# One layer of a streaming encoder in float32: S4 of the Strassen weights by an addition on VectorE, and another order of the down products

## The chip, the cores and the metric

The kernel runs on 1 core of one Trainium2 chip. The metric is the device time of one execution in microseconds (us); the figure that counts is the median over runs. TensorE (PE) multiplies, VectorE (DVE) and ScalarE (ACT) work on elements, GpSimd (POOL) and SyncE (SP) mostly issue transfers here.

## The reference, cut to what matters

One layer on 512 tokens of width 1024: a half-step SwiGLU feed-forward, a mixer (state-space scan and chunked attention), a second half-step feed-forward, a final norm. The change touches the two feed-forwards alone:

```python
def swiglu(h, w_gate, w_up, w_down):
    return (jax.nn.silu(h @ w_gate) * (h @ w_up)) @ w_down

x = x + 0.5 * swiglu(rms_norm(x, ffn1_norm[i]), ffn1_w_gate[i], ffn1_w_up[i], ffn1_w_down[i])
x = x + hybrid_mixer(x, ...)
x = x + 0.5 * swiglu(rms_norm(x, ffn2_norm[i]), ffn2_w_gate[i], ffn2_w_up[i], ffn2_w_down[i])
```

All of it is float32, with 2816 hidden columns.

## The kernel before, in words

**Products.** Every float32 product is made of three TensorE products of a high and a low part (high x high, high x low, low x high). The high part of a weight unit is a cast by ACT (line 272), the low part a subtraction on VectorE (line 274). Both write a ring of four pairs of tiles named xw (`usplit`, lines 267 to 275), so the cast for a unit has to wait until the unit four before it has been multiplied.

**Seven products for eight.** The 2816 hidden columns are cut into 11 blocks d of two tiles. A block's gate and up weights form a 2 x 2 matrix of units A11, A12, A21, A22 of 512 KB each. The first two blocks of the first feed-forward and the first of the second are multiplied plainly (A11 to A22); all others by the Winograd form of Strassen's scheme, with seven products P1 to P7 whose weights are A11 (P1), A12 (P2), A22 (P4), S1 = A21 + A22 (P5), S2 (P6: S1 and A11), A11 and A21 (P7) and S4 (P3: S2 and A12). The signs lie in how the arrays are laid out and in the operands. The down weights go the same way, as units of two blocks, in three groups of blocks: 0 to 3, 4 to 7 and 8 to 10. The first feed-forward does two of these groups so, the second all three.

**Where the sums are made.** `ffn_weights` (line 309) makes a Job for each product: a list of transfers, and a split. A plain unit is loaded by SP into one of four buffers named raw (`whole`, line 323). S1 is loaded by SP into a quarter of the view buffers (tiles s40 and s52; `first`, line 329) and added to by a transfer that POOL issues with an accumulate (`more`, line 332). S2 adds A11 to the same view by another such transfer, after S1 has been split; S4 adds A12 to it by a third, after S2 has been split. P7's weights are made by adding to P1's raw buffer. A12 is thus read twice from memory: once into a raw buffer for P2, and once for S4.

**The order.** `program` (line 281) writes the products out by hand. In the gate/up blocks they are P5, P1 of block d, P3, P4 of block d - 1, P6, P2, P7 of block d. In the down groups 0 and 1 they follow DOWN (line 279), every product as a pair of units, with P3 and P4 of the last gate/up block and P5 and P1 of the next one put between. Each turn calls `Stream.get`, which splits the units up to three products ahead (`look`; two ahead within a pair) and starts transfers whose lead (the numbers 5, 6, 7, 12 in `product`) has come, if the job that has to be split first has been. This is the order of the text; the order on each engine, and the points at which the queues of SP and POOL take a transfer, are set from it by the framework's own plan when the kernel is built.

**What multiplies.** `run` (line 545) does one gate/up product: 24 matmuls of 256 columns (line 555) into one of three PSUM banks of the block: P1, P6, P7 and P4 into X, P2 into L, P5 and P3 into H. After P1 and after P6 ACT copies the bank out (lines 560 and 563), and the next product of that bank waits for it. `down` (line 604) does the down products, 12 matmuls of 512 columns for a unit (lines 142 to 144), and VectorE adds finished banks to x (line 628).

Of the kernel before, what the change touches and what calls it, by code (L numbers as in the profile page):

```python
# [12 lines left out]
ALU = mybir.AluOpType  # L13
# [24 lines left out]
def hybrid_block(ctx: ExitStack, tc, xT, xt, par, wgu1, wd1, ws1, win, wdt, wv, wo, rbt, wgu2, ws2, fin, out):  # L38
    nc = tc.nc
    V, S, G, T = nc.vector, nc.scalar, nc.gpsimd, nc.tensor  # L40
# [4 lines left out]
    def sb(tag, shape, dt=F32, bufs=1):  # L45
        uid[0] += 1
        return pool.tile(shape, dt, tag=tag, name=f"{tag}_{uid[0]}", bufs=bufs)
# [9 lines left out]
    def f(ap):  # L57
        return ap.bitcast(F32)
# [51 lines left out]
    class Stream:  # L110
# [16 lines left out]
        def get(self):  # L127
            i = self.used
            self.used += 1
            while self.done < min(len(self.jobs), i + 1 + self.look):  # L130
                job = self.jobs[self.done]
                job.move(0, True)
                job.parts = job.split()
                self.done += 1
            for n in range(self.done, min(len(self.jobs), i + 18)):
                self.jobs[n].move(n - i)
            return self.jobs[i].parts
# [95 lines left out]
    def wide_tile(g, dt=F32R):  # L233
        if g not in wide or wide[g][0] != dt:
            wide[g] = dt, sb(f"s{g}", [P, GROUPS[g], SEQ], dt)
        return wide[g][1]
# [30 lines left out]
    def usplit(src):  # L267

        i = turn[0] % 4
        turn[0] += 1  # L270
        hi = sb(f"xw{2 * i}", list(src.shape), F32R)
        S.copy(out=hi, in_=src)  # L272
        lo = sb(f"xw{2 * i + 1}", list(src.shape), F32R)
        V.tensor_tensor(out=lo, in0=src, in1=f(hi), op=ALU.subtract)  # L274
        return hi, lo

    DOWN = ("P5", "P1", "P2", "P6", "P7", "P3", "P4")

    def program(plain, by_tokens):


        if plain == 1:
            out = [("A11", 0), ("A21", 0), ("A12", 0), ("P1", 1), ("P5", 1), ("A22", 0), ("P6", 1), ("P2", 1), ("P7", 1)]
        else:
            out = [(a, d) for d in range(plain) for a in ("A11", "A21", "A12", "A22")]
            out += [(p, plain) for p in ("P5", "P1", "P6", "P2", "P7")]
        out = [("P", p, d) for p, d in out]
        ends = [b for _, b in BLOCKS[:2]]  # L290
        for d in range(plain + 1, ND):
            if d - 1 not in ends:
                out += [("P", p, e) for p, e in (("P5", d), ("P1", d), ("P3", d - 1), ("P4", d - 1))]
            out += [("P", p, d) for p in ("P6", "P2", "P7")]
            if d in ends:

                down = [("S", ends.index(d), p, (0, 1)) for p in DOWN]
                out += down[:1] + [("P", p, d) for p in ("P3", "P4")] + down[1:6]
                out += [("P", p, d + 1) for p in ("P5", "P1")] + down[6:]
        last = [("P", p, ND - 1) for p in ("P3", "P4")]  # L300
        if by_tokens == 3:
            return out + [("S", 2, "P5", (0,))] + last + [("S", 2, p, (0,)) for p in ("P1", "P2")] + [
                ("S", 2, p, (1,)) for p in ("P1", "P5")] + [("S", 2, "P6", (0, 1)), ("S", 2, "P2", (1,))] + [
                ("S", 2, p, (0, 1)) for p in ("P7", "P3", "P4")]
        out += [("D", 2, 0, 0)] + last + [("D", 2, 1, 0), ("D", 2, 0, 1), ("D", 2, 1, 1)]
        return out + [("D", 2, o, c) for o in range(2, KD) for c in range(2)]

    def ffn_weights(wgu, plain, by_tokens, wst, wd=None):


        bufs, jobs, views = {}, {}, []
        LAST = (2, ND - 1)

        def view(d):
            if d not in bufs:
                i = views.index(d)
                m = 2 if type(d) is int else min(2, BLOCKS[d[0]][1] - d[1])
                bufs[d] = wide_tile((40, 52)[i // 2 % 2], F32)[:, 2 * (i % 2):2 * (i % 2) + m]
                if type(d) is int:
                    bufs[d] = bufs[d].rearrange("p a (k c) -> p a k c", c=P)  # L320
            return bufs[d]

        def whole(key, src):
            def go():
                bufs[key] = sb("raw", list(src.shape), bufs=4)
                nc.sync.dma_start(out=bufs[key], in_=src)
            return go

        def first(d, src):
            return lambda: nc.sync.dma_start(out=view(d), in_=src)  # L330

        def more(get, src):
            return lambda: G.dma_start(out=get(), in_=src, accum_op=ALU.add)  # L333

        def product(p, d, A):

            sum_ = lambda: view(d)
            raw = {"P1": "g", "P2": "g2", "P4": "u2"}.get(p)
            if p[0] == "A":
                n = ("A11", "A12", "A21", "A22").index(p)  # L340
                j = Job(lambda: usplit(bufs[p, d]), (6, "raw", whole((p, d), A[n])))
            elif raw:
                j = Job(lambda: usplit(bufs[raw, d]), (6 if p == "P1" else 5, "raw",
                                                       whole((raw, d), A[("P1", "P2", "", "P4").index(p)])))
            elif p == "P5":
                views.append(d)
                before = jobs["P3", views[-5]] if len(views) > 4 else jobs.get(("A21", 0))
                j = Job(lambda: usplit(view(d)), (12, before, first(d, A[2])), (7, None, more(sum_, A[3])))
            elif p == "P6" and d == LAST:

                v = d + (2,)
                views.append(v)
                j = Job(lambda: usplit(view(v)), (14, jobs["P3", views[-5]], first(v, A[2])),
                        (10, None, more(lambda: view(v), A[3])), (6, None, more(lambda: view(v), A[0])))
            elif p == "P6":
                j = Job(lambda: usplit(view(d)), (6, jobs["P5", d], more(sum_, A[0])))
            elif p == "P7":
                j = Job(lambda: usplit(bufs["g", d]), (6, jobs["P1", d], more(lambda: bufs["g", d], A[2])))
            else:
                v = d + (2,) if d == LAST else d  # L360
                j = Job(lambda: usplit(view(v)), (6, jobs["P6", d], more(lambda: view(v), A[1])))
            jobs[p, d] = j
            if p == "P7":
                jobs["P1", d].holds = j
            ws.jobs.append(j)

        for step in program(plain, by_tokens):
            if step[0] == "P":
                p, d = step[1:]
                product(p, d, wgu[d])  # L370
            elif step[0] == "S":
                n, p, pieces = step[1:]
                for a in [BLOCKS[n][0] + 2 * c for c in pieces]:
                    product(p, (n, a), [wst[i, :, a:min(a + 2, BLOCKS[n][1]), :] for i in range(4)])
            else:
                n, o, c = step[1:]
                if c == 0:
                    a, b = 2 * BLOCKS[n][0], 2 * BLOCKS[n][1]
                    ws.add(wd[o, :, a:b, :], b - a, P)
                    late = ws.jobs.pop() if (n, o) in ((2, 0), (2, 1)) else None  # L380
                    if late:
                        jobs["late", o] = late
                elif ("late", o) in jobs and n == 2:
                    ws.jobs.append(jobs["late", o])

    class XCombos:
# [40 lines left out]
        def split(self, d, src):  # L427
            S.copy(out=d[0], in_=src)
            V.tensor_tensor(out=d[1], in0=src, in1=f(d[0]), op=ALU.subtract)
# [25 lines left out]
    def ffn(xc, n_plain, early, by_tokens, rc, between, after):  # L455
# [179 lines left out]
        for step in program(n_plain, by_tokens):  # L635
            if step[0] == "S":
# [5 lines left out]
                down(*step[1:])  # L642
                past = step[1:3] == (1, DOWN[-1])
                continue
# [786 lines left out]
```

## Time and profile before

| what | value |
|---|---|
| median of 3 runs | 1032.14 us (1031.85, 1032.14, 1036.27) |
| the profiled execution, its own time | 1035.34 us |
| its span | 1033.6 us |
| TensorE matmul / weight load busy | 1007.9 us (98%) / 888.6 us (86%) |
| VectorE / ACT / POOL busy | 810.2 us (78%) / 587.8 us (57%) / 163.7 us (16%) |
| moved by transfers | 162.66 MB, 60.04 MB of it on the queue that POOL feeds |

The profile is of one execution. Times count from the start of its span. PE rows are matmuls, PEld rows are the weight loads that go beside them. An arrow in brackets names what an engine had waited for. The first feed-forward runs from about 10 to 310 us, the mixer from there to about 660, the second feed-forward to the end.

### The profile page before, as it was taken

How to read it: one execution, taken by the hardware profiler on the slowest of the kernel's cores; microseconds unless marked ns; L12 is line 12 of the kernel's file. 1: busy time of each engine (PE TensorE's matmuls, PEld its weight loads, DVE VectorE, ACT ScalarE, POOL GpSimd, SP SyncE). 2: the span in 40 equal slices, each digit the busy share in tenths (PEclk: the TensorE clock that was granted, in tenths of full speed). 3: DMA queues.
4: the chain of work that ended last, by engine and by line, in shares of the span. 5: the costliest groups of instructions: out<-in, count | busy, mean ns of one | idle time of the engine just before them, and what ended most of it. 6: DMA issues, size and time to landing. Idle time of an engine off the chain costs nothing. (4 is left out here: it accounts for less than half of the span.)

```text
span 1033.6 us, 16129 instructions
## 1 busy us (share of the span) xinstructions
PE 1007.9 (98%) x6154; PEld 888.6 (86%) x6154; DVE 810.2 (78%) x1353; ACT 587.8 (57%) x926; POOL 163.7 (16%) x186
## 2 busy tenths in 40 slices
PE   8999999999999999999999999999999999999895
PEld 7889989998898777778878778879999899988884
DVE  7868876887676698978867999797688668876587
ACT  7555535654474456646656876666655356544445
POOL 1111121111110013323201111101211111111110
PEclk9999999999999999999999999999999999999988
DMA  8969989998652321222232223755898889988842
GB/s 309 290 160 210 218 185 228 224 203 211 147 122 91 102 82 62 71 73 69 71 98 71 82 83 102 230 131 128 191 211 209 196 209 231 209 213 202 167 107 99
DMA packets 48221, 162.66 MB, mean 157 GB/s; under 512 B 5264, under 2 KB 6032, under 8 KB 48144
## 3 DMA queue, kind: packets, MB, share of 16 engines
q0 software_dynamic: 16848, 60.04, 33.2%
q1 hardware_dynamic: 28992, 96.74, 27.1%
q10 hardware_dynamic: 2304, 4.86, 1.5%
q8 instruction: 48, 0.79, 0.3%
q14 instruction: 29, 0.24, 0.1%
HBM read 159.52 MB, written 2.10 MB: 156 GB/s over the span
## 5 line engine op out<-in xcount | busy, mean ns | idle before, releaser
L555 PE MATMUL mm<-s,xw 128*128 128x256 f32 x1824 | 231.6, 284 | 6.4 <-ACT fu L563 4.6
L555 PEld LDWEIGHTS mm<-s,xw 128*128 128x128 f32 x1824 | 224.9, 192 | 7.6 <-ACT fu L563 5.0
L272 ACT CAST xw<-raw 128x1024 fp32r<-128x1024 f32 (+1 forms) x127 | 131.5, 1036 | 138.3 <-PE mm L555 56.0
L274 DVE TENSOR_TENSOR xw<-raw,xw 128x1024 fp32r<-128x1024 f32 (+1 forms) x127 | 152.7, 1204 | 69.4 <-ACT xw L272 69.4
L555 PE MATMUL aux<-s,xw 128*128 128x256 f32 x1368 | 174.5, 283 | 0.6 <-DVE xw L274 0.6
L555 PEld LDWEIGHTS aux<-s,xw 128*128 128x128 f32 x1368 | 169.0, 192 | 1.9 <-DVE xw L274 0.8
L142 PE MATMUL mm<-xw,whi 128*128 128x512 f32 x364 | 149.1, 410 | 0.0
L143 PE MATMUL mm<-xw,whi 128*128 128x512 f32 x364 | 144.3, 397 | 0.0
L274 DVE TENSOR_TENSOR xw<-s,xw 128x1024 fp32r<-128x1024 f32 (+1 forms) x87 | 104.6, 1202 | 50.5 <-ACT xw L272 50.4
L144 PE MATMUL mm<-xw,wlo 128*128 128x512 f32 x364 | 144.0, 396 | 0.0
L272 ACT CAST xw<-s 128x1024 fp32r<-128x1024 f32 (+1 forms) x87 | 90.0, 1035 | 92.1 <-DMA s<-wgu 27.7
L333 POOL DMA_DIRECT2D s<-wgu x57 | 52.1, 934 | 314.6 <-DMA s<-wgu 133.6
L84 ACT CAST whi<-raw 128x512 fp32r<-128x512 f32 (+1 forms) x104 | 62.1, 601 | 65.3 <-PE mm L143 47.2
L86 DVE TENSOR_TENSOR wlo<-raw,whi 128x512 fp32r<-128x512 f32 (+1 forms) x104 | 74.3, 716 | 13.8 <-ACT whi L84 13.2
L142 PEld LDWEIGHTS mm<-xw,whi 128*128 128x128 f32 x364 | 68.5, 188 | 16.2 <-issue 2.2
L144 PEld LDWEIGHTS mm<-xw,wlo 128*128 128x128 f32 x364 | 68.4, 188 | 16.1
L143 PEld LDWEIGHTS mm<-xw,whi 128*128 128x128 f32 x364 | 68.5, 188 | 15.8 <-issue 1.2
L333 POOL DMA_DIRECT2D s<-ws x31 | 27.1, 873 | 163.3 <-DVE xw L274 65.8
L144 PE MATMUL aux<-xw,s 128*128 128x512 f32 x106 | 41.8, 394 | 0.0
L143 PE MATMUL aux<-xw,s 128*128 128x512 f32 x106 | 41.7, 394 | 0.0
L142 PE MATMUL aux<-xw,s 128*128 128x512 f32 x106 | 41.7, 394 | 0.0
L903 POOL TENSOR_TENSOR fu<-dt,tri 128x512 fp32r<-128x512 f32 x16 | 18.9, 1190 | 95.6 <-PE aux L954 45.5
(294 smaller groups left out, 1743.9 us busy)
## 6 DMA issues: line engine op xcount, KB each, us to landing
raw<-wgu SPq DMA_DIRECT2D x68, 512.0 KB, 5.8
s<-wgu POOLq DMA_DIRECT2D x57, 512.0 KB, 6.5
raw<-win SPq DMA_DIRECT2D x28, 512.0 KB, 3.5
s<-ws POOLq DMA_DIRECT2D x27, 512.0 KB, 5.7
raw<-ws SPq DMA_DIRECT2D x27, 512.0 KB, 4.7
s<-wgu SPq DMA_DIRECT2D x19, 512.0 KB, 5.0
raw<-wgu POOLq DMA_DIRECT2D x19, 512.0 KB, 6.2
raw<-wo SPq DMA_DIRECT2D x12, 512.0 KB, 3.7
```

Of the source, the lines that this page charges most:

```text
L84: S.copy(out=hi, in_=src)
L86: V.tensor_tensor(out=lo, in0=src, in1=f(hi), op=ALU.subtract)
L142: T.matmul(ps, lhsT=sh, rhs=mh, start=start, stop=False, skip_group_check=skip)
L143: T.matmul(ps, lhsT=sh, rhs=ml, start=False, stop=False, skip_group_check=skip)
L144: T.matmul(ps, lhsT=sl, rhs=mh, start=False, stop=stop, skip_group_check=skip)
L272: S.copy(out=hi, in_=src)
L274: V.tensor_tensor(out=lo, in0=src, in1=f(hi), op=ALU.subtract)
L333: return lambda: G.dma_start(out=get(), in_=src, accum_op=ALU.add)
L555: T.matmul(ps[:, j * HS:(j + 1) * HS], lhsT=sw[:, j, k], rhs=m, start=(p in ("P1", "P2", "P5") and j == 0 and k == 0 and n == 0), stop=(k ...
L903: G.tensor_tensor(out=r, in0=f(src[:, c, h0:h0 + 4]).unsqueeze(2).broadcast_to([P, 4, P]), in1=tri.unsqueeze(1).broadcast_to([P, 4, P]), o ...
```

## The change

S4's transfer goes for all gate/up blocks done in seven products and for the down groups 0 and 1 (`here`); the down group 2 keeps it. In its place the split of P2 begins with one VectorE addition of the raw buffer, which holds A12, to the view, which holds S2. For this S2 must have been split already, so in DOWN the product P6 goes ahead of P2; in the gate/up blocks it is there already.

```diff
-    DOWN = ("P5", "P1", "P2", "P6", "P7", "P3", "P4")
+    DOWN = ("P5", "P1", "P6", "P2", "P7", "P3", "P4")
...
             sum_ = lambda: view(d)
+            here = type(d) is int or d[0] < 2
             raw = {"P1": "g", "P2": "g2", "P4": "u2"}.get(p)
...
+            elif p == "P2" and here:
+                def split():
+
+                    V.tensor_tensor(out=view(d), in0=view(d), in1=bufs[raw, d], op=ALU.add)
+                    return usplit(bufs[raw, d])
+                j = Job(split, (5, "raw", whole((raw, d), A[1])))
             elif raw:
...
+            elif here:
+                j = Job(lambda: usplit(view(d)))
             else:
                 v = d + (2,) if d == LAST else d
                 j = Job(lambda: usplit(view(v)), (6, jobs["P6", d], more(lambda: view(v), A[1])))
```

## Rows read from the trace of the kernel before

**Rows 1.** The page's busy time of each engine

```profile
PE 1007.9 (98%) x6154; PEld 888.6 (86%) x6154; DVE 810.2 (78%) x1353; ACT 587.8 (57%) x926; POOL 163.7 (16%) x186
```

**Rows 2.** Stretches of 20 us: length, then busy us of each engine, PEclk, DMA share, GB/s

```profile
680.00:700.00 20.00, 19.45 (x100) 16.67 (x101) 19.96 (x38) 10.31 (x17) 1.74 (x2) 1.00 0.44 102
...
860.00:880.00 20.00, 20.00 (x169) 20.00 (x168) 16.38 (x24) 12.14 (x18) 3.52 (x4) 1.00 0.93 214
...
980.00:1000.00 20.00, 17.39 (x100) 16.07 (x101) 14.06 (x23) 10.23 (x16) 1.73 (x2) 0.83 0.51 118
```

**Rows 3.** Waits of TensorE: us in total, times, longest us

```profile
PE mm L555 <- ACT fu L563: 4.6, 1, 4.6
PE mm L555 <- ACT fa L560: 1.8, 1, 1.8
...
PE aux L205 <- DVE s L198: 0.6, 1, 0.6
```

**Rows 4.** Timeline of TensorE near 978: start us, us, line, operation, [idle before]

```profile
957.71 3.04 PE L555 MATMUL mm<-s,xw 128*128 128x256 f32 x24
...
974.93 3.04 PE L555 MATMUL aux<-s,xw 128*128 128x256 f32 x24
982.61 5.24 PE L555 MATMUL mm<-s,xw 128*128 128x256 f32 x24 [4.64 <-ACT fu L563]
```

**Rows 5.** Timeline of ACT in the same stretch

```profile
981.03 1.04 ACT L272 CAST xw<-s 128x1024 fp32r<-128x1024 f32 x1 [6.35 <-DMA s<-wgu]
981.98 0.58 ACT L563 COPY fu<-mm 128x512 f32<-128x512 f32 x1
```

**Rows 6.** Timeline of POOL in the same stretch

```profile
971.52 0.88 POOL L333 DMA_DIRECT2D s<-ws  x1 [3.73 <-DMA s<-ws]
972.14 1.14 POOL L333 DMA_DIRECT2D s<-wgu  x1
```

**Rows 7.** Stretches of 4 us, columns as in the stretches of 20

```profile
60.00:64.00 4.00, 2.21 (x16) 2.01 (x17) 3.97 (x8) 3.00 (x4) 0.00 (x0) 1.00 0.61 174
...
972.00:976.00 4.00, 4.00 (x35) 4.00 (x35) 4.00 (x9) 2.49 (x5) 1.90 (x3) 1.00 0.79 160
...
980.00:984.00 4.00, 1.39 (x6) 1.39 (x7) 1.89 (x3) 2.97 (x4) 0.00 (x0) 0.57 0.37 73
```

**Rows 8.** The page's transfers: a queue, and issues with us to landing

```profile
q0 software_dynamic: 16848, 60.04, 33.2%
...
s<-wgu POOLq DMA_DIRECT2D x57, 512.0 KB, 6.5
```

**Rows 9.** Timeline of VectorE near 978

```profile
959.24 1.22 DVE L274 TENSOR_TENSOR xw<-s,xw 128x1024 fp32r<-128x1024 f32 x1
```

**Rows 10.** Timeline of VectorE, opening of the first feed-forward

```profile
58.70 1.22 DVE L274 TENSOR_TENSOR xw<-raw,xw 128x1024 fp32r<-128x1024 f32 x1
59.84 0.42 DVE L494 TENSOR_TENSOR fa<-fh,fh 128x256 f32<-128x256 f32 x1
```

**Rows 11.** Waits of VectorE

```profile
DVE xw L274 <- ACT xw L272: 119.8, 89, 5.8
```

**Rows 12.** Timeline of ACT, opening of the first feed-forward

```profile
53.75 1.05 ACT L272 CAST xw<-s 128x1024 fp32r<-128x1024 f32 x1 [7.15 <-DMA s<-wgu]
...
60.29 0.62 ACT L477 CAST s<-fa 128x512 fp32r<-128x512 f32 x1 [1.06 <-DVE fa L494]
...
62.71 0.58 ACT L560 COPY fa<-mm 128x512 f32<-128x512 f32 x1
```

**Rows 13.** Timeline of TensorE, opening of the first feed-forward

```profile
59.97 1.58 PE L555 MATMUL aux<-s,xw 128*128 128x256 f32 x11 [0.63 <-DVE xw L274]
63.34 3.13 PE L555 MATMUL mm<-s,xw 128*128 128x256 f32 x24 [1.79 <-ACT fa L560]
```

**Rows 14.** Timeline of VectorE, opening of the second feed-forward

```profile
699.93 0.15 DVE L169 TENSOR_TENSOR rq_q<-rq_o 128x4 f32<-128x4 f32 x1
...
700.81 0.68 DVE L198 TENSOR_TENSOR s<-ident,rq_h 128x512 fp32r<-128x512 f32 x1
```

## The prediction

> **What bounds the kernel now.** I read the busy shares first: TensorE has work in 98% of the span, VectorE in 78% [rows 1]. A share of 98% can still hide slow feeding, so I read the stretches of 20 us next. From 860 to 880 TensorE and its weight load are both busy for 20.00 of 20 us, beside a DMA share of 0.93; from 680 to 700 and from 980 to 1000 TensorE lacks time, and in the last the granted clock is 0.83 [rows 2]. So a steady gate/up stretch has nothing to give, however many transfers are taken out of it, and what this change can win lies in a few holes. The waits of TensorE name them: one of 4.6 us on ACT's copy of line 563, one of 1.8 us on ACT's copy of line 560, one of 0.6 us on the VectorE work of line 198 [rows 3]. The timeline then says what each hole is made of.
>
> The largest is at the end of the second feed-forward. Products follow each other every 2.87 us (six from 957.71 to 974.93); P2 of column block 10 runs from 974.93, and P7 of 10 should follow near 977.9 but starts at 982.61, and its 24 matmuls then take 5.24 us instead of 3.04 [rows 4]. ACT explains it: the copy that frees P6's bank for P7 starts at 981.98, behind a cast that waited 6.35 us for a transfer into a view buffer [rows 5]. By the order of the splits in the code (P2's turn splits the third product ahead) this cast is that of P3 of 10, and the transfer is the very accumulation that makes S4. POOL issued it at 972.14, queued behind an accumulation for the down weights that waited for its own first transfer until 971.52 [rows 6]. The cast could start 8.9 us later.
>
> **What it costs.** The wait is 4.64 us. The slow matmuls cost another 5.24 - 3.04 = 2.20 us, at a granted clock of 0.57 from 980 to 984 (between the levels of 1.2 and 2.4 GHz) [rows 4, 7]. Together 6.84 us.
>
> **The change part by part.**
>
> *Removed:* the S4 accumulations, one for each gate/up block done in seven products (9 + 10) and one for each of eight units of down blocks 0 and 1: 27 of 512 KB. Of 57 accumulations from the gate/up weights 19 go [rows 8]. They are 14.2 of the 60.0 MB on the software queue, whose packets take 33.2% of the engines' time [rows 8]: about 8 points of DMA share. In the steady stretches that buys nothing, by rows 2. In the hole at 978 it takes away the transfer that ACT waits for: **-6.84 us**. What is late next there? P3's cast then needs only P2's addition. VectorE is busy for 4.00 of 4 us from 972 to 976 [rows 7], so at worst the addition comes behind that burst and leaves a hole of about 1.2 us; at best none. I take none, since the addition stands in the text ahead of P2's own split.
>
> *Added:* 27 additions of 128x1024 on VectorE. The nearest row is the split's subtraction of the same shape: 1.22 us alone, 1.14 us from start to start when another follows [rows 9, 10]. That is 27 x 1.14 to 1.22 = 31 to 33 us of VectorE time, to be hidden. The cover in steady stretches: VectorE idles 119.8 us in 89 places before the subtraction because ACT's cast is still running, 1.35 us each [rows 11], and the addition needs no cast, so it fits there. Where it does not fit there is lead: a subtraction that starts at 959.24 and ends at 960.46 belongs to the product three ahead of the one that starts at 957.71 [rows 4, 9], so of the one at 957.71 + 3 x 2.87 = 966.32, and 5.9 us are spare. Two additions in a row, as in the down blocks, take 2.4 of these. Cost there: nothing.
>
> *Where the cover is gone.* Two places have no idle VectorE.
> - The opening of the first feed-forward. VectorE is busy for 3.97 of 4 us from 60 to 64 [rows 7]. P6 of block 2 waits for ACT's copy at 62.71, which stands on ACT behind a cast (60.29) that waited for VectorE's instruction of line 494 [rows 12, 10]; TensorE waits 1.79 us [rows 13]. P2's addition stands in the text ahead of line 494's, so I move the whole queue by one addition: +1.14 us. Bounds: -1.8 us (the engines' order falls out better and the hole closes) to +3.3 us (1.14 us and the 2.20 us of a fallen clock).
> - The opening of the second. The chain of short operations for the norm runs bare on VectorE from 699.93 on [rows 14], and TensorE waits 0.6 us for its end [rows 3]. The addition can be put between two of them: 0 to +1.14 us, I take half, +0.6.
>
> *New waits.* The addition waits for A12's load; behind it on VectorE stand P2's subtraction and the reads of PSUM by which banks come free. That load waited on its cast before, so it is no later than it was. The cast of P3 now waits for VectorE instead of a transfer, two or more products after the addition.
>
> *Moved.* In the down blocks the P2 pair goes behind the P6 pair: P6's two accumulations on POOL are due two products earlier, P2's two loads on SP as much later, and the banks of P2 are taken and given back later. No wait of TensorE lies in these stretches before [rows 3], and a like sum takes 6.5 us to land [rows 8], against a lead of six products. POOL's queue is passed by nothing that is due sooner. Cost: nothing; bounds 0 to +1.
>
> **The sum** on the profiled execution: -6.84 + 1.14 + 0.6 = -5.1 us, so 1035.34 becomes 1030.2. That execution was 3.2 us above the median of 1032.14, and the runs shown (1031.85, 1032.14, 1036.27) lie at two heights about 4 us apart. If the 3.2 us are part of the hole at 978, a median run has only 3.6 us of it to lose and ends at 1030.2; if they lie elsewhere, it ends at 1027.0. I cannot tell which, and take the middle: **1028.6 us**, with 1026 to 1031 as this case's own range. A measurement of this kernel tells 0.5% (5.2 us) from no change, so the bounds are 1027.0 and 1037.3, and the forecast itself straddles the first.
>
> **A rule against the change.** The trace shows that a hole can be paid for twice: after 4.64 us of waiting the next 24 matmuls ran at a granted clock of 0.57, but from 60 to 64, with waits of 0.63 and 1.79 us, it stayed at 1.00 [rows 7, 13]. The Trainium skill (TensorE: Matmul & The Clock Gate, "What's actually happening") says that the half rate is TensorE's default, from which only activity releases it. By that page a hole that an addition widens may bring the fall along, and the opening of the first feed-forward would then cost an estimated 1.14 + 2.20 = 3.3 us; by the rows so far, 1.14 us. The trace agrees with the page at 978 and shows no fall at 60.
>
> **The rivals.**
> - *The additions meet a saturated VectorE, and the clock falls with the holes they widen* (slower). Place: the two openings. Price: 1.14 + 2.20 us at each, 6.7 us. It decides if the hole at 978 is hardly there in a median run, so that nothing pays for it: 1032.14 + 6.7 = 1038.8. For it: VectorE's 19.96 of 20 us at 680 to 700 [rows 2]. Against: both openings' holes are short so far, and the profile does show the hole at 978. Chance 0.10.
> - *The hole is only handed on.* The next instruction on ACT or VectorE holds the copy up, or another accumulation comes late behind POOL's queue, as this one did [rows 6]. Then -6.84 is given back: 1032.14 to 1034. For it: the order on each engine is not the text's, as P2's 11 matmuls at 59.97 ahead of P6's at 63.34 show [rows 13], so a new order comes with the change. Chance 0.25.
> - *Every hole in the feed-forwards closes*, the 1.79 and 0.63 us too, because less traffic lets P6's sum land sooner: 1032.14 - 6.84 - 2.4 = 1022.9. Against: the late sum there (ACT waits 7.15 us for it at 53.75 [rows 12]) is due before any removed transfer. Chance 0.07.
> - *The change doesn't take the transfers away.* The code leaves no move for P3 where the new case holds, so this has no chance worth naming.
>
> **The numbers.** Forecast 0.58, handed on 0.25, slower 0.10, all closed 0.07. Of the forecast's 0.58 some 0.24 lies below 1027.0. Faster: 0.24 + 0.07 = 0.31. Slower: 0.10. Same: 0.59. The range reaches from 1024 (the forecast with the full hole and no new cost at the openings is 1025.3, and a part of the case in which all closes) to 1035 (the hole handed on, with a bound of 1 us for the moved pair); outside lie most of the slower case and half of the fastest, under 2 in 10.
>
> **What would show it.** Right: 38 accumulations from the gate/up weights instead of 57; no TensorE wait of over 1.2 us near 978 and a granted clock of 1.00 there; VectorE busy for 841 to 843 us; the wait on line 560's copy near 2.9 us; steady stretches still at 20.00 of 20. Wrong: a new TensorE wait of several us behind ACT or VectorE in the down blocks or at an opening, with a granted clock under 1 behind it; or the same hole at 978 with another releaser.

## The result, and the profile after

The median fell from 1033.7 us (9 runs, 1031.85 to 1036.27) to **1028.3 us** (9 runs, 1026.99 to 1029.49): a measured ratio of 0.994, with a 95% interval from 0.9928 to 0.9952 (the two medians alone divide to 0.9948, inside it). The profiled execution took 1027.64 us (span 1025.9) against 1035.34 us (1033.6) before, so 7.7 us of span are to be found. In the kernel after, line 555 has become 564, 560 is 569, 563 is 572, and the addition is line 346.

The page of the kernel after: busy time, a queue, the addition's group, and the accumulations from the gate/up weights.

```profile
PE 1006.1 (98%) x6154; PEld 887.0 (86%) x6154; DVE 841.3 (82%) x1380; ACT 588.3 (57%) x926; POOL 140.2 (14%) x159
...
q0 software_dynamic: 12960, 45.88, 25.9%
...
L346 DVE TENSOR_TENSOR s<-s,raw 128x1024 f32<-128x1024 f32 x27 | 33.0, 1222 | 0.6
...
s<-wgu POOLq DMA_DIRECT2D x38, 512.0 KB, 5.6
```

VectorE has 31.1 us more than in [rows 1], 27 instructions, 33.0 us by the group. The software queue is 14.2 MB lighter than in [rows 8], and 38 accumulations stand where 57 stood. Now the waits of the kernel after (us in total, times, longest), TensorE's and VectorE's:

```profile
PE mm L564 <- ACT fa L569: 1.2, 1, 1.2
...
PE aux L205 <- DVE s L198: 0.6, 1, 0.6
...
DVE xw L274 <- ACT xw L272: 83.9, 81, 6.1
```

The longest wait of [rows 3], 4.6 us on the copy of line 563, has no successor: nothing waits on line 572. VectorE's idle places ahead of the subtraction hold 83.9 us instead of the 119.8 of [rows 11]: 35.9 us less, about the 33.0 that the additions take.

The end of the second feed-forward in the timeline of the kernel after (start, us, engine, line, operation, idle before and what ended it), by engine:

```profile
968.61 5.87 PE L564 MATMUL mm<-s,xw 128*128 128x256 f32 x48
974.31 3.04 PE L564 MATMUL aux<-s,xw 128*128 128x256 f32 x24
977.19 3.04 PE L564 MATMUL mm<-s,xw 128*128 128x256 f32 x24
980.07 0.40 PE L142 MATMUL aux<-xw,s 128*128 128x512 f32 x1
...
974.45 1.05 ACT L272 CAST xw<-s 128x1024 fp32r<-128x1024 f32 x1 [0.39 <-PE mm L564]
975.40 0.58 ACT L572 COPY fu<-mm 128x512 f32<-128x512 f32 x1
...
965.31 1.23 DVE L346 TENSOR_TENSOR s<-s,raw 128x1024 f32<-128x1024 f32 x1
```

P2 of block 10 runs at 974.31 and P7 follows after 2.88 us, without a wait and in 3.04 us. ACT's cast of P3 waits 0.39 us, for a ring buffer, where it waited 6.35 us for a transfer [rows 5]; the copy behind it is done before P2 is. The addition ran at 965.31, nine microseconds ahead of that cast, before VectorE's burst. The stretches of the kernel after (length, busy us of PE, PEld, DVE, ACT, POOL with counts, granted clock, DMA share, GB/s):

```profile
980.00:984.00 4.00, 4.00 (x23) 3.35 (x23) 2.67 (x4) 2.96 (x4) 0.89 (x1) 1.00 0.24 66
980.00:1000.00 20.00, 20.00 (x111) 17.23 (x111) 17.24 (x28) 10.51 (x16) 3.48 (x4) 1.00 0.62 134
860.00:880.00 20.00, 20.00 (x170) 20.00 (x169) 17.37 (x25) 11.93 (x17) 2.60 (x3) 1.00 0.79 184
```

The clock is 1.00 from 980 on, where [rows 7] had 0.57. The steady stretch is at 20.00 as before, with 1 us more of VectorE and a DMA share of 0.79 instead of 0.93 [rows 2]: lighter, and no shorter.

The opening of the first feed-forward, in the same timeline, and one line of the opening of the second:

```profile
52.91 1.05 ACT L272 CAST xw<-s 128x1024 fp32r<-128x1024 f32 x1 [5.72 <-DMA s<-wgu]
...
62.07 0.58 ACT L569 COPY fa<-mm 128x512 f32<-128x512 f32 x1
...
56.34 1.22 DVE L346 TENSOR_TENSOR s<-s,raw 128x1024 f32<-128x1024 f32 x1
...
59.55 1.97 PE L564 MATMUL aux<-s,xw 128*128 128x256 f32 x13
62.70 3.13 PE L564 MATMUL mm<-s,xw 128*128 128x256 f32 x24 [1.19 <-ACT fa L569]
...
699.44 1.23 DVE L346 TENSOR_TENSOR s<-s,raw 128x1024 f32<-128x1024 f32 x1
```

P6 of block 2 starts at 62.70 instead of 63.34 [rows 13]. POOL's issue of the accumulation that P6's sum waits for, in the kernel after and then in the kernel before, and the matmul behind P7 of block 10 in the kernel before:

```profile
44.96 0.87 POOL L333 DMA_DIRECT2D s<-wgu  x1 [1.00 <-DVE fa L509]
```

```profile
44.37 0.88 POOL L333 DMA_DIRECT2D s<-wgu  x1 [0.57 <-DVE fa L500]
...
987.69 0.39 PE L142 MATMUL aux<-xw,s 128*128 128x512 f32 x1
```

**Where the 7.7 us are**, by starts of the same matmuls in both traces: the kernel after is 0.6 us behind when it comes to this opening (53.80 for 53.20), 0.64 ahead at P6, 0.62 ahead still in the last blocks (957.09 for 957.71), 5.42 ahead at P7 of block 10 (977.19 for 982.61) and 7.62 ahead right behind it (980.07 for 987.69). So TensorE wins 1.24 us over the opening, nothing at the second opening, and 4.80 + 2.20 = 7.0 us at the hole. The 0.6 us behind is there from the first products on: TensorE waits 0.99 us for ACT's line 149 at 8.84 us, before 0.39 us. It costs nothing in the end, since P6 waits for its sum anyway; against the kernel before the opening is worth 0.64 us.

### The profile page after: what moved, and what is told of

It is laid out like the page before. It is cut to its first block, busy times and chain, and to the rows that moved or that the text cites. A ratio compares the mean times of both kernels' runs of the same rounds, so it can differ in the third digit from the quotient of the medians.

```text
span 1025.9 us, 16097 instructions
## 1 busy us (share of the span) xinstructions
PE 1006.1 (98%) x6154; PEld 887.0 (86%) x6154; DVE 841.3 (82%) x1380; ACT 588.3 (57%) x926; POOL 140.2 (14%) x159
## 4 chain that ended last, share of the span: by engine, by line
PE 82%; DVE 10%; DMA 3%; ACT 2%; issue 1%; POOL 0%; SPq 0%; ACTq 0%; POOLq 0%; DVEq 0%
PE mm L564 21%; PE aux L564 16%; PE mm L142 10%; PE mm L143 10%; PE mm L144 10%; PE aux L144 3%; PE aux L143 3%; PE aux L142 3%; DMA s<-wgu 2%; DVE fs L857 2%; DVE wlo L86 1%; DMA raw<-wgu 1%; DVE xw L274 1%; PE aux L981 1%; PE aux L772 1%
## 5 line engine op out<-in xcount | busy, mean ns | idle before, releaser
L333 POOL DMA_DIRECT2D s<-wgu x38 | 33.6, 898 | 361.7 <-DMA s<-wgu 115.3
L333 POOL DMA_DIRECT2D s<-ws x23 | 20.0, 869 | 137.1 <-DMA s<-ws 71.4
L346 DVE TENSOR_TENSOR s<-s,raw 128x1024 f32<-128x1024 f32 x27 | 33.0, 1222 | 0.6
```

The source lines that it names most:

```text
L346: V.tensor_tensor(out=view(d), in0=view(d), in1=bufs[raw, d], op=ALU.add)
```

## The experiments

My theory after reading both traces: the whole gain is one transfer of 27, S4 of block 10 in the second feed-forward, and that one only because of its place on POOL's queue. The rivals: less traffic as such; the new order of the down products; and VectorE's additions as a cost hidden in the net.

**The addition for one product alone.** The kernel before, with the new case for block 10 of the second feed-forward only, and DOWN as it was:

```diff
-    DOWN = ("P5", "P1", "P6", "P2", "P7", "P3", "P4")
+    DOWN = ("P5", "P1", "P2", "P6", "P7", "P3", "P4")
...
-            here = type(d) is int or d[0] < 2
+            here = plain == 1 and d == ND - 1
```

> The kernel before, with S4 by addition in one place alone: gate/up block 10 of the second feed-forward (DOWN as before, the other 26 transfers kept). Theory (the gain is the one hole at the end of the second feed-forward, made by this one transfer): 4 to 6 us below the kernel before, a ratio of 0.994 to 0.996; no TensorE wait on the copy of P6's bank near 978, clock 1.00 there. Rival (the gain is 14.2 MB less traffic, spread over 27 transfers): 5.4 / 27 = 0.2 us, a ratio of 1.000.

**All but that one.** The kernel after, with the transfer kept there alone:

```diff
-            here = type(d) is int or d[0] < 2
+            here = (type(d) is int or d[0] < 2) and not (plain == 1 and d == ND - 1)
```

> The changed kernel, with the transfer kept in that one place (block 10 of the second feed-forward) and the other 26 taken away. Theory: the hole near 978 comes back with 2 to 5 us of waiting, and the time is within 1.5 us of the kernel before (ratio 0.998 to 1.001). Rival (traffic): 26/27 of the gain, a ratio of 0.994.

Measured: one addition gives 1027.9 us (1026.82 to 1029.92; before 1035.14 on that chip), ratio 0.9934 [0.9918, 0.995]. Twenty-six additions without it give 1034.72 us, ratio 1.0 [0.9987, 1.0012]. The timeline with one addition (P7 of block 10), then with all but one (P7, and POOL ahead of it):

```profile
979.36 3.04 PE L564 MATMUL mm<-s,xw 128*128 128x256 f32 x24
```

```profile
980.74 4.38 PE L564 MATMUL mm<-s,xw 128*128 128x256 f32 x24 [3.51 <-ACT fu L572]
...
969.92 0.86 POOL L333 DMA_DIRECT2D s<-ws  x1 [3.79 <-DMA s<-ws]
970.54 1.12 POOL L333 DMA_DIRECT2D s<-wgu  x1
```

One transfer of 27 carries the gain; the other 26, or the traffic that they are, give nothing that can be measured. With one addition the time fell by 7.2 us, more than the 4 to 6 expected.

The two runs also tell what the addition does at the first opening, where the run with all but one has it and the run with one addition has not. The waits of P2 and P6 there, with one addition and then with all but one, and in the latter ACT's cast of the sum and its copy of line 569:

```profile
59.41 1.57 PE L564 MATMUL aux<-s,xw 128*128 128x256 f32 x11 [0.46 <-DVE xw L274]
62.77 4.63 PE L564 MATMUL mm<-s,xw 128*128 128x256 f32 x24 [1.79 <-ACT fa L569]
```

```profile
60.24 1.57 PE L564 MATMUL aux<-s,xw 128*128 128x256 f32 x11 [1.15 <-DVE xw L274]
63.00 3.13 PE L564 MATMUL mm<-s,xw 128*128 128x256 f32 x24 [1.18 <-ACT fa L569]
...
53.22 1.05 ACT L272 CAST xw<-s 128x1024 fp32r<-128x1024 f32 x1 [6.87 <-PE mm L144]
62.37 0.58 ACT L569 COPY fa<-mm 128x512 f32<-128x512 f32 x1
```

With the sum's cast as late as without the change (53.22, though its row names TensorE and not the transfer for the end of its wait; 53.18 with one addition), the addition moves P2's wait up by 0.7 us and P6's down by 0.6. From the cast to the copy it is 62.37 - 53.22 = 9.15 us, against 8.96 with one addition and 8.96 in the kernel before [rows 12].

**The transfers kept, POOL's order changed.** If the place on the queue is the cause, no addition is needed at all. The kernel before, with one edge of order: the accumulation that starts the sum of the last down unit is issued behind the S4 accumulation of block 10.

```diff
-        def more(get, src):
-            return lambda: G.dma_start(out=get(), in_=src, accum_op=ALU.add)
+        def more(get, src, keep=None, behind=None):
+            def go():
+                if behind and behind in kept:
+                    with tc.issue_after(kept[behind]):
+                        G.dma_start(out=get(), in_=src, accum_op=ALU.add)
+                else:
+                    kept[keep] = G.dma_start(out=get(), in_=src, accum_op=ALU.add).ins
+            return go
+
+        kept = {}
...
-                        (10, None, more(lambda: view(v), A[3])), (6, None, more(lambda: view(v), A[0])))
+                        (10, None, more(lambda: view(v), A[3], behind=("P3", ND - 1))), (6, None, more(lambda: view(v), A[0])))
...
-                j = Job(lambda: usplit(view(v)), (6, jobs["P6", d], more(lambda: view(v), A[1])))
+                j = Job(lambda: usplit(view(v)), (6, jobs["P6", d], more(lambda: view(v), A[1], keep=("P3", d))))
```

> The kernel before with all its transfers; one edge added: POOL issues the first accumulation for the third view of the last down unit behind the S4 accumulation of block 10, which had stood behind it. Theory (the hole is made by the transfer's place on POOL's queue, not by the transfer): S4 is issued near 966 and lands by 975, the hole shrinks to under 1 us, and the time is 4 to 6 us below the kernel before (0.994 to 0.996). Rival (traffic, or the transfer as such): 1.000, with the hole still there.

Measured: 1028.48 us (1026.14 to 1030.06), ratio 0.9938 [0.9922, 0.9954], as the changed kernel's 0.994, and 6.7 us less than the kernel before on that chip (4 to 6 were expected). Its timeline, POOL and P7 of block 10 (line 555 is 563 there, 333 is 336 and 338):

```profile
966.49 0.88 POOL L338 DMA_DIRECT2D s<-wgu  x1 [7.82 <-DVE xw L274]
967.40 0.88 POOL L336 DMA_DIRECT2D s<-ws  x1
...
978.00 3.04 PE L563 MATMUL mm<-s,xw 128*128 128x256 f32 x24
```

The S4 transfer, issued at 966.49, no longer stands behind the accumulation that held it until 972.14 [rows 6], and the hole is gone with all 57 transfers in place: P7 starts without a wait and takes 3.04 us. That is the cause, shown by taking it away without the addition.

**The kernel before, once more.** To see how steady the hole is.

> The kernel before once more, for a second profile. If the spread of its runs (1031.85 to 1036.27) lies in the hole, this execution's time less its hole (the wait on the copy of P6's bank and the matmuls behind it that run slow) is 1027.5 to 1029.5, as 1035.34 - 6.84 = 1028.5 was, whatever the time itself. If the spread lies elsewhere, the hole is 4 to 5 us again and the rest differs.

1036.82 us. Its timeline at the first opening and at P7 of block 10, and a stretch at the opening:

```profile
59.96 1.57 PE L555 MATMUL aux<-s,xw 128*128 128x256 f32 x11 [0.58 <-DVE xw L274]
63.33 4.57 PE L555 MATMUL mm<-s,xw 128*128 128x256 f32 x24 [1.79 <-ACT fa L560]
...
983.97 5.49 PE L555 MATMUL mm<-s,xw 128*128 128x256 f32 x24 [4.69 <-ACT fu L563]
```

```profile
64.00:68.00 4.00, 4.00 (x23) 4.00 (x22) 1.60 (x3) 0.85 (x2) 0.88 (x1) 0.57 0.70 172
```

The hole is 4.69 + (5.49 - 3.04) = 7.1 us here, and the time without it 1029.7 us, just above the 1027.5 to 1029.5 expected if the whole spread lay in the hole. New is a second loss: with the same two waits as in [rows 13], P6 of block 2 took 4.57 us instead of 3.13, at a granted clock of 0.57. So these two executions of one kernel differ by that fall too, 1.4 us.

**The down blocks alone.** The kernel after, with the additions in the down groups 0 and 1 and nowhere else; the new DOWN stays.

```diff
-            here = type(d) is int or d[0] < 2
+            here = type(d) is not int and d[0] < 2
```

> The change in the down blocks alone: P6 ahead of P2 and 8 additions there, the 19 transfers of the gate/up blocks kept. Theory (nothing waits in the down blocks): the hole near 978 as before, a ratio of 0.998 to 1.002. Rival (the new order of the down products, or 8 transfers less, has a part in the gain, or a cost that the rest hides): off 1.000 by 0.002 or more.

1034.11 us (12 runs), ratio 1.0006 [0.9994, 1.0018]. Eight additions and the moved pair cost nothing and bring nothing, to about 0.12%. In the profile the hole is there (wait 3.8, P7 in 5.49 us), and so is the clock fall at the opening.

**More work on VectorE.** Behind each addition one more instruction of its shape that leaves the values as they are, then three of them:

```diff
                     V.tensor_tensor(out=view(d), in0=view(d), in1=bufs[raw, d], op=ALU.add)
+                    V.tensor_tensor(out=view(d), in0=view(d), in1=view(d), op=ALU.max)
                     return usplit(bufs[raw, d])
```

> The changed kernel, with every addition followed by a second VectorE instruction of the same size on the same view (the maximum of the view with itself, which leaves it as it is): 27 x 1.2 = 33 us more VectorE work, 874 us busy. Theory (additions are hidden behind TensorE, and 5.9 us of lead take what doesn't fit the idle places): at most 1.5 us above the changed kernel, at the opening (a ratio of 0.993 to 0.996). Rival (the first addition had used the cover up): a third or more of the 33 us shows, a ratio over 1.004.

> The changed kernel, with three such instructions behind every addition: 99 us more VectorE work. A steady gate/up stretch then has 17.37 + 3 x 1.22 = 21.0 us of VectorE work in 20 us. Theory (VectorE binds only past 20 of 20): 10 to 35 us above the changed kernel, with TensorE waiting on line 274 in the steady stretches. Rival (the lead, or moving work about, hides this as well): under 5 us.

One more: 1030.72 us (10 runs), ratio 0.9965 [0.9951, 0.9978], 2.4 us over the changed kernel's median from another series; I had expected at most 1.5. Its stretches and its timeline:

```profile
64.00:68.00 4.00, 3.54 (x17) 3.54 (x18) 3.31 (x7) 1.02 (x2) 0.86 (x1) 0.57 0.60 185
860.00:880.00 20.00, 20.00 (x169) 20.00 (x168) 18.41 (x25) 11.84 (x18) 2.63 (x3) 1.00 0.77 187
```

```profile
61.70 1.58 PE L565 MATMUL aux<-s,xw 128*128 128x256 f32 x11 [2.45 <-DVE xw L274]
64.46 4.54 PE L565 MATMUL mm<-s,xw 128*128 128x256 f32 x24 [1.17 <-ACT fa L570]
```

Three more: 1044.48 us in a single execution, 16 us over the changed kernel, with this steady stretch, this longest group of waits, and one of the three waits with the matmuls behind it:

```profile
860.00:880.00 20.00, 20.00 (x170) 20.00 (x169) 19.97 (x27) 12.11 (x17) 3.49 (x4) 1.00 0.78 189
```

```profile
PE mm L566 <- DVE xw L274: 7.3, 3, 2.6
...
972.38 4.20 PE L566 MATMUL mm<-s,xw 128*128 128x256 f32 x22 [2.64 <-DVE xw L274]
```

In the stretch from 860 to 880 VectorE goes from 17.37 to 18.41 to 19.97 of 20 us, and TensorE stays at 20.00 each time. With one more, the opening of the first feed-forward pays, as the prediction said, only that it takes a second instruction for it: the wait on the subtraction grows to 2.45 us and the clock falls behind it. The profiled execution is the slowest of the ten (1032.26 us), so the median's 2.4 us need not be made up as this picture is. With three, VectorE is full and TensorE stops for it inside gate/up stretches too: at 170.69, 847.76 and 972.38 us, for 2.1 to 2.6 us each, with slow matmuls behind.

**The opening fed in time.** What is left in the changed kernel is the late sum of P6 at the opening. Four loads of x (2 MB, on ACT's queue, issued from 20.36 to 27 us) go out ahead of it, at a time when the transfer engines are full (a share of 0.95 to 1.05 from 24 to 40 us). They are moved behind ACT's copy of line 569, here in the changed kernel:

```diff
-                S.copy(out=e["a"], in_=ps)
+                copies.append(S.copy(out=e["a"], in_=ps).ins)
...
+    copies = []
...
-            S.dma_start(out=x[:, 2 * i:2 * i + 2], in_=xt[:, 2 * i:2 * i + 2])
+            with tc.issue_after(copies[-1]):
+                S.dma_start(out=x[:, 2 * i:2 * i + 2], in_=xt[:, 2 * i:2 * i + 2])
```

> The changed kernel, with the four loads of the transposed x (2 MB) put behind ACT's copy of line 569 in the opening of the first feed-forward, instead of about 20 us into the span. Theory (what is left at the opening is P6 of block 2 waiting for a sum that lands late because those loads fill the transfer engines from 20 to 40 us): the sum's cast starts before 52 us instead of 52.9, TensorE's waits at 58 to 63 go under 0.6 us, no clock falls there, and the time is 0.5 to 2.5 us below the changed kernel, 1025.8 to 1027.8 (a ratio of 0.992 to 0.9945 to the kernel before). Rival (VectorE's queue is what holds the opening, whose busy time there is 4.00 of 4 us): the waits stay at 1.2 us and the time at 1028.3.

1026.37 us (1026.12 to 1026.83), ratio 0.9929 [0.9915, 0.9943]. Its timeline, and one stretch in it and in the kernel after:

```profile
50.53 1.05 ACT L272 CAST xw<-s 128x1024 fp32r<-128x1024 f32 x1 [3.27 <-DMA s<-wgu]
...
61.32 3.14 PE L564 MATMUL mm<-s,xw 128*128 128x256 f32 x24
```

```profile
44.00:52.00 8.00, 8.00 (x37) 6.64 (x36) 6.16 (x13) 4.71 (x9) 1.74 (x2) 1.00 0.56 87
```

```profile
44.00:52.00 8.00, 8.00 (x37) 6.60 (x37) 5.71 (x12) 3.17 (x7) 1.74 (x2) 1.00 1.04 197
```

With the engines' share down from 1.04 to 0.56 in the stretch in which the sum is under way, its cast starts 2.4 us earlier and TensorE waits for neither P2 nor P6. The loads of x don't meet the sum itself, which is issued at 44.96 us; what they held up stands ahead of it on POOL: the accumulation two places before it is issued at 36.51 instead of 41.72 us. About 1 us of that is paid back ahead of it, in a new wait at line 205 (1.1 us).

**The same without any addition.** The two edges of order, on POOL and on ACT, in the kernel before; and the changed kernel with the late loads again, on the same chip.

> The kernel before with two edges of order and no addition: the last down unit's first accumulation behind block 10's S4 on POOL, and the four loads of x behind ACT's first copy of P1's bank. My theory (the additions buy nothing but the place on POOL's queue): the hole near 978 is gone and the waits near 60 are gone, so the same time as the changed kernel with the late loads, 1025.5 to 1027.5, ratio to before 0.991 to 0.994; 57 accumulations, VectorE at 810. Rival (19 transfers fewer are worth something of their own once the opening is fed in time, or the three transfers for S4 weigh on the opening): 1028.5 to 1030.

> The changed kernel with the late loads of x, again, beside the one without additions on the same chip. My theory: 1026.0 to 1027.0 as it was, and within 1 us of the other. Rival (additions worth something of their own): 2 us or more below the other. Second rival (additions cost something at the openings): 1 us or more above it.

Measured: 1026.82 us (1026.07 to 1027.46), ratio 0.9922 [0.9905, 0.994], without additions; 1026.58 us (1025.1 to 1028.21), ratio 0.992 [0.9903, 0.9937], with them. The kernel without additions, page and timeline:

```profile
PE 1005.7 (98%) x6154; PEld 886.5 (86%) x6154; DVE 809.5 (79%) x1353; ACT 587.7 (57%) x926; POOL 164.7 (16%) x186
...
s<-wgu POOLq DMA_DIRECT2D x57, 512.0 KB, 6.4
```

```profile
61.35 3.13 PE L563 MATMUL mm<-s,xw 128*128 128x256 f32 x24
...
976.29 3.04 PE L563 MATMUL mm<-s,xw 128*128 128x256 f32 x24
```

The medians are 0.24 us apart, well inside their ranges. Twenty-seven additions against nineteen transfers from the gate/up weights and eight from the down weights: the exchange itself is worth nothing that can be told here, either way. All three runs with the late loads (1026.37, 1026.82, 1026.58) lie 1.5 to 1.9 us under the changed kernel's 1028.3, but that comes from another series and the intervals of the ratios overlap, so by how much they beat it is not shown. The kernel before they beat clearly.

## Why the prediction was right or wrong

**The hole at 978: right, in place, mechanism and size.** -6.84 us was forecast, 7.0 us came. The prediction named the cast, the transfer and the queue that held it. It treated the cause as "the transfer is removed"; the runs say more narrowly that its place on the queue was the cause, since one edge of order does the same. Nothing was late next, as taken.

**The steady stretches: right.** That 14 MB fewer buy nothing where TensorE is at 20.00 of 20 is borne out by the run with 26 of the 27 exchanges (a ratio of 1.0, to about 0.12%).

**The additions hidden: right.** They lie in the places that the prediction named (119.8 to 83.9 us of idle time), and a second one each is still free in the steady stretch.

**The first opening: the step that failed.** "I move the whole queue by one addition: +1.14 us" was wrong in its path. The addition costs P6 0.2 us: from the cast of the sum to ACT's copy it is 62.07 - 52.91 = 9.16 us instead of 62.71 - 53.75 = 8.96, and 9.15 in the run with all but one, against 8.96 to 8.97 in the four other profiles of this opening without it (one addition, down blocks alone, POOL's order, the repeat). The addition, at 56.34, does put P2's subtraction off, by 0.8 us behind the cast of the sum (5.77 us instead of 4.95; that it starts at 58.68 as before, 58.70 [rows 10], is because the cast was earlier). But ACT's casts took another order, and the copy for P6 hardly moved.

The rest of the difference is not the addition's: the sum's cast starts 0.84 us sooner, 7.95 us after POOL's issue at 44.96, before 9.38 us after the one at 44.37. Together P6 starts 0.64 us earlier, where 1.14 later was forecast (bounds -1.8 to +3.3). No removed transfer is due before it, so this is not the change's by design; in the run with all but one, which has the addition and every other exchange at this opening, the cast is as late as before. Why it landed sooner is open. The run with POOL's order alone, which has nothing of the change here, shows it too (its cast starts 7.19 us after the issue, and P6 waits 0.50 us), so it differs from one kernel to the next; the two profiles of the kernel before agree. That what fills the transfer engines ahead of it can move it is shown by the late loads of x.

The wait on ACT's first copy, forecast near 2.9 us, is 1.2, and 1.18 with the sum as late as before: the same step, since P2's wait takes up what the addition puts off.

**The second opening: +0.6 forecast, nothing came.** The addition was put between two short operations at 699.44, as the prediction had it, and moved the rest of the chain on. But TensorE was given eight matmuls of lines 142 to 144 (from 699.53) ahead of line 205 instead of three, so its wait stayed at 0.6 us. An order of the other engine was not considered.

**The moved pair: right,** nothing (1.0006, to 0.12%).

**The sum and the median.** On the profiled execution -5.1 was forecast and -7.7 came. Of the 2.6 us between them 1.14 + 0.64 = 1.8 lie at the first opening, 0.6 at the second and 0.2 in the hole. The median fits better (1028.6 against 1028.3), and that was luck twice over: the middle between two guesses took another 1.6 us off, and the start was 1.6 us too low, 1032.14 from three runs where nine give 1033.7. The fall that was forecast is 3.5 us, the measured one 5.4. What the guess was about is now known in part: over four profiles with the hole, wait and slow matmuls together measured 6.8, 7.1, 6.3 (down blocks alone) and 4.9 us (all but one), and the clock fall at the opening, 1.4 us, came in two of these and not in the other two. So the spread lies partly in the hole, partly outside it, as far as four profiles tell. The nine runs fill the space between the two heights that the prediction saw in three. The mean granted clock noted for each run goes with its time: of 49 runs of the kernel before on three chips, the 12 at 0.992 or less have a median of 1035.9 us, the 9 at 0.995 or more one of 1032.3. So much of the spread goes with the clock; behind which waits it fell in each run is not recorded.

**The chances.** Within 0.5% was given the most; the ratio of 0.994 is 0.6% faster, with an interval that reaches from just under the bound to 0.72%. The forecast stood on the bound, as it said. That it came out on the far side, and only just, has to do with the kernel before, whose median is 1033.7 over nine runs and not the 1032.14 of three. Of the rivals, the handed-on hole and the saturated VectorE are ruled out for this kernel; the second is real one to three instructions further on. The one in which every hole closes was half right: the sum can land sooner, and with the late loads it does (1026.4), but the change does not bring that about.

## What to carry to other kernels

A transfer can be late for its place on the issuing engine's queue alone (972.14 us there, 966.49 with one edge of order): look at what the issuing engine waited for just before it, and try such an edge before replacing the transfer by work elsewhere. In stretches where the bound engine has no idle time, neither traffic taken away nor work added beside it showed in the time, until the other engine was full itself; count a change only at the holes, and check each of them separately, since here one instance of 27 carried everything. Where several engines' orders are planned anew by the change, a price found by pushing one engine's old queue along is no forecast: here 1.14 us became 0.2.

## What was not expected of the hardware

The same two waits of TensorE at the first opening, 0.46 to 0.63 us and then 1.79 or 1.80 us, left the granted clock at 1.00 in the first profile of the kernel before and brought it down in three others (the repeat, one addition, down blocks alone), where the next 24 matmuls took 4.53 to 4.63 us instead of 3.13. The stretch that shows it lies behind the second wait: in the repeat it is 0.57 from 64 to 68 us, and in the first profile it is 1.00:

```profile
64.00:68.00 4.00, 4.00 (x34) 3.82 (x32) 2.11 (x4) 2.19 (x4) 0.88 (x1) 1.00 0.72 173
```

The prediction read its 1.00 from 60 to 64 us [rows 7], where the repeat has 1.00 as well; its conclusion holds, but not by that row. Waits of 1.15 and 1.18 us (all but one) left the clock up, of 2.45 and 1.17 us (one more instruction) brought it down. So the clock can fall behind waits this short, for 1.4 us, and need not. The Trainium skill (TensorE: Matmul & The Clock Gate, "What's actually happening") calls the throttled rate the default, which activity lifts; the falls in the three profiles (4.53 to 4.63 us) agree with it, and the first profile shows none (3.13 us). The fall that the prediction set against its rows, as an estimate by that page, is thus real there, though smaller (1.4 us, not 2.2). What decides between the two outcomes is open.

The spread of the changed kernel with late loads was 0.7 us in one series and 3.1 us in the next, on two chips with the same code; a narrow spread in six runs is no property of a kernel.
